# A scaled batched matmul with an addend: the last store moves into SyncE's list, and the program is closed while stores are in flight

## The chip, the cores and the metric

The kernel runs on one core of a Trainium2 chip. A core has five engines with an instruction stream each: TensorE (PE in the profile), VectorE (DVE), ScalarE (ACT), GpSimd (POOL) and SyncE (SP), which here does nothing but issue transfers and wait. Sixteen DMA engines move data between the memory of the chip and the core's SBUF. The streams meet only through semaphores. The metric is the device time of one execution in microseconds (us), as the median of several runs; lower is better.

## The reference

```python
def setup_inputs():
    batch, m, k, n = 16, 512, 1024, 768
    ...

def reference(x, weight, scale, add_value):
    return (scale * np.matmul(x, weight) + add_value).astype(np.float32)
```

All arrays are float32: `x` is 16x512x1024, `weight` 1024x768, `add_value` and the output 16x512x768, and `scale` is 0.1.

## The kernel before

The 16x512 rows are taken as one matrix of 8192 rows, cut into 64 tiles of 128 rows. `STREAM` lists, in the order in which SyncE issues them, loads of the weight (`w`), loads of `x` tiles (`x`), loads of addend tiles (`a`) and stores of finished tiles (`o`); an entry gives the first tile and the number of tiles. `sync_engine` walks this list. Ahead of each transfer, `need` puts a wait if SyncE hasn't yet waited for that value: for slots of `x` to be used up, for the store that leaves an addend slot free, or, ahead of a store, for VectorE's count of finished tiles, `made` (L140).

ScalarE and GpSimd (`mover`, L149 to L161) cast `x` to bfloat16 and lay it out, VectorE (`turn`, L171) transposes it, TensorE (`tensor_engine`, L216) multiplies it with the weight, which VectorE has cast, and VectorE (`finish`, L181) scales the product, adds the addend in place in `ao` and raises `made`. `ao` has 32 tile slots; a store reads straight from it. Each engine waits on semaphores whose values are written out by hand, so the order of the work is fixed by the kernel and not by a scheduler.

Two semaphores, `o_sem[0]` and `o_sem[1]`, are used for the stores in turn: store number i raises `o_sem[i % 2]` by 16 when it has landed, and from the third on it first waits until the store two places before it has (L139). The list ends with the stores of tiles 32 to 47 (6144 KB) and of tiles 48 to 59 (4608 KB). GpSimd issues three further, small stores of two tiles in the middle of the run (`store_pair`).

All this stands in one hand-ordered section (`tc.tile_critical`, L240). At its end the framework puts a meeting: SyncE raises a flag, each other engine drains, answers, and SyncE goes on when all have answered. Only then does SyncE issue the last store, of tiles 60 to 63 (1536 KB, `LAST`, L251 and L252), outside the section, with a semaphore that the framework chooses.

The framework's close follows, in a block of instructions of its own (shown as line 283, the launch's `with` statement). SyncE waits for the last store, the five engines meet at a barrier, GpSimd clears the semaphores of the program in one instruction, and the engines meet at a second barrier. There the program ends. Nothing waits by itself for the store of tiles 48 to 59.

Of the kernel before, what the change touches and what calls it, by code (L numbers as in the profile page):

```python
# [21 lines left out]
STREAM = [  # L22
# [5 lines left out]
]  # L28
FIRST, LAST = (0, 8), (60, 4)
PAIR, TURN_AT = slice(8, 16, 7), 2  # L30
BY_POOL = [(122, 6), (0, 98), (98, 24)]

# [2 lines left out]
def kernel(  # L35
# [8 lines left out]
    nc = tc.nc  # L44
# [14 lines left out]
    out_v = out_f.rearrange("(g p t) n -> p g t n", p=P, t=R)  # L59
    w_v = weight.rearrange("(c p r) n -> p c (r n)", p=P, r=2)  # L60

    def rows(view, s, n):
        assert s // R == (s + n - 1) // R
        return view[:, s // R, s % R:s % R + n, :]
# [5 lines left out]
    ao = const.tile([P, A_SLOTS, N], fp32, name="ao")  # L70
# [2 lines left out]
    xt = const.tile([P, XT_TILES, KC, P], fp32, name="xt")  # L73
    mm = psum.tile([P, MM_BUFS, 1024], fp32, name="mm")

    w_sem = [tc.alloc_semaphore(f"w{i}") for i in range(2)]
    x_sem = [tc.alloc_semaphore(f"x{i}") for i in range(X_SLOTS // MOVE)]
    a_sem = tc.alloc_semaphore("a")
    o_sem = [tc.alloc_semaphore(f"o{i}") for i in range(2)]
# [8 lines left out]
    def slot(t):  # L88
        return t % A_SLOTS
# [5 lines left out]
    def sync_engine(eng):  # L95
        groups, stores, known = 0, [], {}

        def need(sem, value):
            if known.get(sem, 0) < value:
                eng.wait_ge(sem, value)  # L100
                known[sem] = value

        for at, (op, s, n) in enumerate(STREAM):
            if at == SYNC_AT:
                eng.addr_align(HALF_BLOCK, offset=PAST, max_nops=0)
            last = s + n - 1
            if op == "w":
                dst = ao[:, W_AT + s:W_AT + s + n, :].rearrange("p (c r) n -> p c (r n)", r=2)
                move, sem = eng.dma_start(dst, w_v[:, s // 2:(s + n) // 2, :]), w_sem[s // 4]
            elif op == "x":  # L110
                k = s % X_SLOTS
                if last >= X_SLOTS:
                    moved = 8 * (last + 1 - X_SLOTS) // MOVE
                    need(by_act, moved)
                    need(by_pool, moved)
                move = eng.dma_start(xs[:, k:k + n, :], rows(x_v, s, n))  # L116
                sem = x_sem[k // MOVE]
            elif op == "a":
                if groups:
                    need(a_sem, 16 * groups)  # L120
                if last == A_SLOTS - 1:
                    need(casts, KJ)
                if s <= PAIR.start + A_SLOTS <= last:
                    need(aside_sem, 16 * len(BY_POOL))
                if s >= A_SLOTS:
                    i = next(j for j, (a, b) in enumerate(stores) if a <= last - 1 - A_SLOTS < a + b)
                    need(o_sem[i % 2], 16 * (i // 2 + 1))
                move = eng.dma_start(ao[:, slot(s):slot(s) + n, :], rows(add_v, s, n))  # L128
                sem = a_sem
                groups += 1  # L130
            elif op == "a+":
                need(a_sem, 16 * groups)
                eng.sem_inc(a_sem, 16 * (n // G - 1))
                groups += n // G - 1
                continue
            else:
                i = len(stores)
                if i > 1:
                    need(o_sem[i % 2], 16 * (i // 2))  # L139
                need(made, MADE + last + 1)  # L140
                move = eng.dma_start(rows(out_v, s, n), ao[:, slot(s):slot(s) + n, :])
                sem = o_sem[i % 2]
                stores.append((s, n))
            move.then_inc(sem, 16)
            if op == "x" and n == 2 * MOVE:
                eng.sem_inc(x_sem[k // MOVE + 1], 16)
# [69 lines left out]
    def tensor_engine(eng):  # L216
        eng.sem_inc(x_sem[1], 16)
        eng.sem_inc(turned, TURNED)
        eng.sem_inc(made, MADE)
        eng.wait_ge(casts, KJ)  # L220
        with eng.Fori(TURNED + 2, TURNED + 2 + T, XT_TILES) as i:
            for q in range(XT_TILES):
                if q % 2 == 0:
                    eng.wait_ge(turned, i + q if q else i)
                    eng.wait_ge(made, i + q if q else i)
                for j in range(KJ):
                    x2 = xt[:, q, j // 2, :].bitcast(bf16).rearrange("p (m r) -> p r m", r=2)
                    m = product(eng, mm[:, q, :], x2[:, j % 2, :], w_bf[:, j, :], j)
                if q % 2:
                    m.then_inc(done, 4)  # L230
# [4 lines left out]
    s, n = FIRST  # L235
# [4 lines left out]
    with tc.tile_critical(no_gpsimd_drain=True):  # L240
        sync_engine(nc.sync)
        mover(nc.scalar, nc.scalar.copy, 0, by_act)
        mover(nc.gpsimd, nc.gpsimd.tensor_copy, 1, by_pool, pool_go, 0, TURN_AT)
        nc.gpsimd.wait_ge(made, MADE + PAIR.stop)
        for p, n in BY_POOL:
            store_pair(nc.gpsimd, p, n)
        nc.gpsimd.addr_align(HALF_BLOCK, offset=PAST, max_nops=0)
        mover(nc.gpsimd, nc.gpsimd.tensor_copy, 1, by_pool, pool_go, TURN_AT, T // X_SLOTS - TURN_AT)
        vector_engine(nc.vector)
        tensor_engine(nc.tensor)  # L250
    s, n = LAST  # L251
    nc.sync.dma_start(rows(out_v, s, n), ao[:, slot(s):slot(s) + n, :])  # L252


# [33 lines left out]
```

## Time and profile before

| | |
|---|---|
| median of 3 runs | 208.18 us (208.1 to 208.29) |
| profiled execution, its own time | 208.1 us |
| span of that execution, first to last instruction | 206.3 us |
| TensorE busy | 168.5 us (82%) |
| GpSimd / ScalarE / VectorE busy | 137.4 / 134.7 / 98.0 us |
| moved by DMA | 87.04 MB, 422 GB/s over the span |
| mean granted TensorE clock | 0.981 |

The span counts from the first instruction of the program; all times of the trace are us from there. An engine's name with a q behind it (SPq, POOLq) means an instruction that its sequencer carries out by itself: a wait, a drain, a branch, the issue of a transfer. `L141` is line 141 of the kernel before. "To landing" is the time from the issue of a transfer until its semaphore has its full count. In a row of the view of windows stand the stretch, its length, busy time and instructions of each engine, then the granted clock, the mean busy share of the 16 DMA engines and GB/s. In a row of the view of one line stand the operation and count, its shortest, median and longest time in ns, and the start of the first and the last of them.

### The profile page before, as it was taken

To read this page: it belongs to the slowest core of one execution; us is meant where nothing else is said; L and a number is where in the kernel's file an instruction comes from. 1 tells how busy PE (TensorE), PEld (TensorE's weight loads), DVE (VectorE), ACT (ScalarE), POOL (GpSimd) and SP (SyncE) were. 2 spreads that over 40 slices of the span, in tenths; PEclk is the share of its full clock that TensorE was granted. 3 is DMA by queue.
4 is the path that set the end of the run, shared out by engine and by line. 5 is a ranking of instruction groups with operands and counts; after the bars stand their busy time and mean duration, and the time that the engine had idled before them with its cause. 6 is when DMAs were issued, how large, how long until landed. Compare 5 with 4: busy or idle time off the path is not lost.

```text
span 206.3 us, 2222 instructions
## 1 busy us (share of the span) xinstructions
PE 168.5 (82%) x1008; PEld 50.5 (24%) x512; DVE 98.0 (48%) x66; ACT 134.7 (65%) x129; POOL 137.4 (67%) x135
## 2 busy tenths in 40 slices
PE   0000099999999999999999999999999999999800
PEld 0000023322333333223333322233333222333200
DVE  0005523555555555555555555555554655455320
ACT  2049970799999807999999069999990199910000
POOL 0049994699999906999999459999991199920000
PEclk9999999999999999999999999999999999999975
DMA  7989999999999999999999999999999999999986
GB/s 299 413 378 467 400 483 407 419 438 464 407 457 457 407 407 407 407 457 408 437 434 423 447 424 434 432 419 443 438 415 429 429 437 443 429 457 419 457 367 281
DMA packets 4065, 87.04 MB, mean 422 GB/s; under 512 B 480, under 2 KB 480, under 8 KB 1120
## 3 DMA queue, kind: packets, MB, share of 16 engines
q1 hardware_dynamic: 3856, 86.25, 97.7%
q0 software_dynamic: 208, 0.79, 0.9%
q14 instruction: 1, 0.01, 0.0%
HBM read 61.87 MB, written 25.17 MB: 422 GB/s over the span
## 4 chain that ended last, share of the span: by engine, by line
DMA 37%; PE 37%; POOL 10%; ACT 5%; issue 4%; DVE 2%; SPq 1%; POOLq 0%; DVEq 0%; ACTq 0%
PE mm L208 37%; DMA out_dram<-ao 22%; DMA xs<-in_x_dram 15%; POOL va L161 9%; ACT va L161 5%; DVE xt L176 1%; DVE ao L185 1%; POOL out_dram L93 1%; SPq L128 0%; SPq L116 0%; DVEq L174 0%; SPq L100 0%; POOLq L154 0%; POOLq L151 0%; DVEq L185 0%
## 5 line engine op out<-in xcount | busy, mean ns | idle before, releaser
L208 PE MATMUL mm<-w_bf,xt 128*128 128x256 bf16 (+1 forms) x1008 | 168.5, 328 | 27.1 <-DVE xt L176 26.2
L161 POOL CAST va<-xs 32x1024 bf16<-32x1024 f32 x128 | 135.2, 1056 | 44.3 <-DMA xs<-in_x_dram 30.6
L161 ACT CAST va<-xs 32x1024 bf16<-32x1024 f32 x128 | 133.4, 1042 | 45.3 <-DMA xs<-in_x_dram 41.7
L185 DVE SCALAR_TENSOR_TENSOR ao<-mm,ao 128x1536 f32 (+1 forms) x32 | 56.2, 1757 | 76.7 <-PE mm L208 73.6
L206 PEld LDWEIGHTS <-xt 128*128 128x128 bf16 x512 | 50.5, 99 | 144.5 <-issue 117.6
L176 DVE STREAM_TRANSPOSE xt<-va 128x1024 f32<-128x1024 f32 x32 | 39.4, 1234 | 4.6 <-POOL va L161 2.4
L169 DVE CAST w_bf<-ao 128x3072 bf16<-128x3072 f32 x2 | 4.6, 2276 | 18.0 <-DMA ao<-in_weight_dram 18.0
L150 ACT ACT_TABLE_LOAD x1 | 1.3, 1283 | 1.3 <-SPq L240 1.3
L93 POOL DMA_DIRECT2D out_dram<-ao x3 | 2.0, 672 | 0.0
L269 POOL MEMSET const-float32-0.0<- 128x1 f32 x1 | 0.1, 97 | 0.2 <-issue 0.2
L269 POOL MEMSET const-bfloat16-1.0<- 128x1 bf16 x1 | 0.1, 100 | 0.0
L269 POOL MEMSET const-float32-1.0<- 128x1 f32 x1 | 0.1, 98 | 0.0
L269 POOL MEMSET const-uint8-127<- 128x1 uint8 x1 | 0.1, 98 | 0.0
## 6 DMA issues: line engine op xcount, KB each, us to landing
xs<-in_x_dram SPq DMA_DIRECT2D x7, 4096.0 KB, 20.9
ao<-in_add_value_dram SPq DMA_DIRECT2D x6, 3072.0 KB, 16.0
out_dram<-ao SPq DMA_DIRECT2D x3, 3072.0 KB, 27.4
ao<-in_add_value_dram SPq DMA_DIRECT2D x1, 6144.0 KB, 24.2
out_dram<-ao SPq DMA_DIRECT2D x1, 6144.0 KB, 31.2
out_dram<-ao SPq DMA_DIRECT2D x1, 4608.0 KB, 14.7
xs<-in_x_dram SPq DMA_DIRECT2D x2, 2048.0 KB, 21.1
ao<-in_weight_dram SPq DMA_DIRECT2D x2, 1536.0 KB, 16.8
```

The lines of the kernel that those rows point to most:

```text
L93: eng.dma_start(out_v[p:p + n, 0, PAIR, :], ao[p:p + n, PAIR, :]).then_inc(aside_sem, 16)
L150: eng.preload_act_table(mybir.ActivationFunctionType.Copy)
L161: copy(va[q % VA_BUFS][32 * b:32 * b + 32, :, a, :], src[32 * a:32 * a + 32, :, b, :]).then_inc(count, 1)
L169: eng.tensor_copy(w_bf[:, s:s + n, :], ao[:, W_AT + s:W_AT + s + n, :]).then_inc(casts, n)
L176: eng.transpose(xt[:, 2 * half:2 * half + 2, :, :].rearrange("p i c m -> p (i c m)"), va[move % VA_BUFS][:, q:q + 2 * KC, :, :].bitcast(fp ...
L185: eng.scalar_tensor_tensor(a, mm[:, q:q + 2, 0:N], float(scale), a, op0=mybir.AluOpType.mult, op1=mybir.AluOpType.add).then_inc(made, 2)
L206: eng.ldweights(x_j, tile_position=(0, 0))
L208: m = eng.add_instruction(mybir.InstMatmult(start_tensor_calc=(j == 0), stop_tensor_calc=(j == KJ - 1), tile_size=(P, P), tile_position=(0 ...
L269: nc = _bacc.Bacc("TRN2", target_bir_lowering=False, num_devices=1)
```

## The change

The last store becomes an entry of `STREAM`. The last two stores of the list, those from tile 48 on, raise a new semaphore, `ending`, that is not one of the framework's. Behind the section the kernel itself closes its pools, closes the context and compiles the program, and then adds one instruction to SyncE: wait until `ending` has reached 32, and take 32 off it.

```diff
     ("x", 60, 4), ("a", 56, 8), ("o", 32, 16), ("o", 48, 12),
+    ("o", 60, 4),
 ]
-FIRST, LAST = (0, 8), (60, 4)
+FIRST, ENDING = (0, 8), 48
...
+    end_sem = nc.alloc_semaphore("ending")
     w_sem = [tc.alloc_semaphore(f"w{i}") for i in range(2)]
...
                 need(made, MADE + last + 1)
                 move = eng.dma_start(rows(out_v, s, n), ao[:, slot(s):slot(s) + n, :])
-                sem = o_sem[i % 2]
+                sem = o_sem[i % 2] if s < ENDING else end_sem
                 stores.append((s, n))
...
         tensor_engine(nc.tensor)
-    s, n = LAST
-    nc.sync.dma_start(rows(out_v, s, n), ao[:, slot(s):slot(s) + n, :])
+    ctx.close()
+    tc.close()
+    tc.compile()
+    ending = 16 * sum(op == "o" and s >= ENDING for op, s, n in STREAM)
+    nc.sync.wait_ge(end_sem, ending).then_inc(end_sem, -ending)
```

In the built program the instructions of TensorE, VectorE, ScalarE and GpSimd are the same ones in the same order; the numbers of the semaphores shift by one, and GpSimd's clearing covers all but `ending`. On SyncE the last store stands inside the section, behind one wait for `made` and a wait of its own for `o_sem[0]` to reach 48, which is the landing of the store of tiles 32 to 47. The wait for the last store ahead of the first closing barrier is gone; the wait for `ending` stands behind the second.

## The prediction

> **What bounds the kernel now.** I read the page first, for the share of each engine, the transfer rates and the chain of waits.
>
> ```profile
> span 206.3 us, 2222 instructions
> DMA packets 4065, 87.04 MB, mean 422 GB/s; under 512 B 480, under 2 KB 480, under 8 KB 1120
> q14 instruction: 1, 0.01, 0.0%
> DMA 37%; PE 37%; POOL 10%; ACT 5%; issue 4%; DVE 2%; SPq 1%; POOLq 0%; DVEq 0%; ACTq 0%
> ```
>
> No engine is full; DMA moves 422 GB/s on average and shares the chain with TensorE. The change lies at the end, so I then followed the chain of waits in order of time to its last piece, the timeline of SyncE, and every DMA issue with its time to landing.
>
> ```profile
> 195.63 1.76 DVE ao L185
> ...
> 159.69 27.67 SPq L141 DMA_DIRECT2D out_dram<-ao  x2
> 197.67 0.33 SPq L252 DMA_DIRECT2D out_dram<-ao  x1
> ...
> 187.01 0.34 SPq L141 DMA_DIRECT2D out_dram<-ao  x1
> ...
> out_dram<-ao SPq DMA_DIRECT2D x1, 6144.0 KB, 31.2
> out_dram<-ao SPq DMA_DIRECT2D x1, 4608.0 KB, 14.7
> out_dram<-ao SPq DMA_DIRECT2D x1, 1536.0 KB, 7.7
> ```
>
> The chain stops at the last piece of compute, 195.63 + 1.76 = 197.39 us. The 8.9 us from there to 206.3 are the last store and the close, and the chain shows neither. The merged row of two stores starts at the first of them, 159.69; the second is the row at 187.01. So the last three stores land at 159.69 + 31.2 = 190.9, 187.01 + 14.7 = 201.7 and 197.67 + 7.7 = 205.4 us. What follows 205.4 is the closing code, line 283:
>
> ```profile
> L283 POOLq EVENT_SEMAPHORE  x4: 17/17/17, 205.6 to 206.2; - x4
> L283 SPq EVENT_SEMAPHORE  x3: 17/17/17, 205.4 to 206.2; - x3
> L283 PEldq EVENT_SEMAPHORE  x2: 51/51/51, 205.7 to 206.3; - x2
> L283 POOLq EVENT_SEMAPHORE_RANGE_CLEAR  x1: 161/161/161, 205.9 to 205.9; - x1
> ...
> SPq L283 <- DMA out_dram<-ao: 7.4, 1, 7.4
> ```
>
> SyncE waits 7.4 us for the last store (197.67 + 0.33 + 7.4 = 205.4). Only then do the five engines meet, GpSimd clears the semaphores (161 ns), they meet again, and the last of them, TensorE's, finishes at 206.3. So 206.3 - 205.4 = 0.9 us of closing stand behind the landing with nothing else running.
>
> **The close goes under the store.** In the changed kernel the same meeting, clearing and meeting are issued with both stores in flight, and SyncE alone waits behind them on a semaphore that the clearing leaves out. The closing work is the same, 0.9 us. Ahead of it stands the end of the hand-ordered section, whose length is the time from the last compute to the old store issue, 197.67 - 197.39 = 0.28 us: SyncE raises a flag, the others drain and answer. Before, that flag went up at 187.4; now it goes up behind the last issue, so the other four engines stand idle until then, with nothing left to do. The new order ends near 197.8 + 0.3 + 0.9 = 199.0 us, with 205.4 - 199.0 = 6.4 us to spare. What hides the close is the flight of the last store; with that cover gone it would cost its 0.9 us again, plus the 0.28. Removed from the path: 0.9 us.
>
> **Does the close really not wait for transfers?** The drains are what could. The trace has SyncE's drain standing right behind an issue, with that store in flight:
>
> ```profile
> L240 SPq DRAIN  x1: 53/53/53, 187.5 to 187.5; - x1
> ```
>
> It took 53 ns at 187.5, behind the issue of 187.01 to 187.35, and that store landed at 201.7. So a drain waits for the issue and not for the landing. I take zero; the other bound, a drain that holds to the landing, gives back the whole 0.9.
>
> **The last store's issue.** It now stands in SyncE's list. It waits for the last compute, then for the 6144 KB store, since two stores share each of the semaphores in turn, then it goes. The second wait was met at 190.9, 6.5 us before the first. Two rows of the chain price a wait instruction ahead of a transfer:
>
> ```profile
> 116.72 0.02 SPq L100
> 116.74 0.03 issue
> 116.77 0.38 SPq L116
> ```
>
> That is 0.05 us. A store that waits for compute directly went at 187.01, and its compute ended at 185.23 + 1.76 = 186.99, so 0.02 us of reaction. The new issue is at 197.39 + 0.02 + 0.05 = 197.46, 0.21 us earlier than 197.67. Behind the waiting store stands only the close, so nobody else is held.
>
> ```profile
> 185.23 1.76 DVE L185 SCALAR_TENSOR_TENSOR ao<-mm,ao 128x1536 f32<-128x1536 f32 x1 [1.99 <-PE mm L208]
> ```
>
> **What the earlier issue is worth.** Here I had to choose. Between the landings at 190.9 and 201.7, 4608 KB went out in 10.8 us, which is 437 GB/s; between 201.7 and 205.4, 1536 KB in 3.7 us, 425 GB/s. Both are the mean rate of the whole run (422) or above it. So the three stores run nose to tail through a full pipe. I checked whether the last one could have started sooner, by the first load of the program, issued at 0.74 us:
>
> ```profile
> 0.74 0.38 SPq L237 DMA_DIRECT2D xs<-in_x_dram  x1
> ...
> 0.74:1.50 0.76, 0.00 (x0) 0.00 (x0) 0.00 (x0) 0.16 (x1) 0.00 (x0) 1.00 0.00 0
> 1.50:2.00 0.50, 0.00 (x0) 0.00 (x0) 0.00 (x0) 0.50 (x1) 0.00 (x0) 1.00 2.05 590
> ...
> 199.60:199.80 0.20, 0.00 (x0) 0.00 (x0) 0.00 (x0) 0.00 (x0) 0.00 (x0) 0.50 2.56 1106
> 200.20:200.40 0.20, 0.00 (x0) 0.00 (x0) 0.00 (x0) 0.00 (x0) 0.00 (x0) 0.50 0.00 0
> ```
>
> The last two columns are the DMA share and GB/s. Nothing moved until 1.50 and packets began before 2.00, so an issue takes 0.76 to 1.26 us to its first packet. The last store was ready by 197.67 + 1.26 = 198.9 at the latest, yet was served from about 201.7 - 205.4: it stood 2 to 3 us in line. An empty window at 200.20 seems to speak against a full pipe. It doesn't: a share of 2.56 in 0.2 us is possible only if a packet's whole time is booked at its start, so empty windows are those in which no packet begins. Issuing 0.21 us earlier therefore lengthens the time in line, from 7.7 to about 7.9 us, and the landing stays at 205.4. What hides this part is the 4608 KB store ahead. I take 0 for it, between 0 and a gain of 0.21.
>
> The Trainium skill ("DMA: Bandwidth & Descriptors", in "Anatomy of one DMA") fits a transfer by itself as 2.0 us plus its bytes at 436 GB/s. By that estimate the last store would take 5.6 us, be bound by its issue and carry the 0.21 us to the end, for a gain of 1.1; the measured 7.7 us says that it waited about 2 us for others, so here the trace decides against it.
>
> **The new last wait.** One semaphore instruction of SyncE, 17 ns as in the row of line 283. Its count is 32, both stores; the 4608 KB one lands 3.7 us before the other, so it is never the later. Before, no wait was spent on it at all.
>
> **What lies around the span.** The profiled execution took 208.1 us, 1.8 more than its span, and the trace doesn't show how that is made up. The last engine still has to finish and report, so I leave the 1.8 as it is; the bounds are no change and one meeting of the engines saved, because four of them arrive early: half of the 0.9, 0.45 us.
>
> **Sum**, against the profiled execution: 208.1 - 0.9 (close) - 0 (issue) + 0.02 (wait) = 207.2 us. The median of the runs shown, 208.18, is 0.08 above that execution, so the forecast is 207.3 us, 0.4% faster. A change of less than 0.2%, 0.42 us, can't be told from none.
>
> **Rivals.**
>
> *The landing follows the issue.* If the DMA engines did run dry before the last store, its landing moves with the issue, to 205.2, and the gain is 0.9 + 0.21: 207.1 us. For it: the empty window at 200.20 if it is taken at its word. Against: the rates between the landings.
>
> *The time around the span shrinks as well.* Four engines stop near 199 us rather than at 206.3. If a meeting behind the program costs less for that, 0.45 more is saved: 206.85 us. Nothing in the trace speaks for or against.
>
> *The change doesn't do what it says.* If a drain or the clearing holds until the stores have landed, the 0.9 us stay behind the landing and SyncE's 0.02 comes on top: 208.2 us, no change. Against: the drain of 53 ns.
>
> *Slower: the closing code isn't there when it is wanted.* One mechanism: the jump into the closing block has to fetch its instructions through the same DMA engines, behind two stores. A small transfer in a full pipe can take long:
>
> ```profile
> out_dram<-ao POOLq DMA_DIRECT2D x1, 144.0 KB, 18.6
> ```
>
> A fetch held until the pipe empties arrives at 205.4, and the chain of 0.28 + 0.9 = 1.2 us then ends at 206.6, 0.3 later than before: 208.5, still within what can't be told. From a second fetch in series on, 1.0 us or so by the load at 0.74 us (between 0.76 and 1.26), it is slower: 209.5. For a single fetch, it decides when it takes over 6.4 us. For it: the closing code stands in a block of its own, reached by a jump. Against: the page has one instruction packet in the whole run, and ScalarE made the same jump in 0.1 us, from its drain at 187.4 to the one behind it at 187.5:
>
> ```profile
> L240 ACTq DRAIN  x1: 8/8/8, 187.4 to 187.4; - x1
> L283 ACTq DRAIN  x2: 8/8/8, 187.5 to 205.8; - x2
> ```
>
> The Trainium skill ("Runtime: NRT & Kernel Launch", in "Instruction fetch mechanics") says that a taken branch to a target outside the two blocks held forces a fetch by DMA before the engine goes on. By that rule the jump could stall; ScalarE's 0.1 us says that here the target was held.
>
> **How the numbers follow.** Forecast 68%, with a range of its own of 207.1 to 207.5 (rounding of 0.9 to a tenth, and the spread of the runs, 0.19 us). Landing follows the issue 12%, time around the span shrinks 7%, no change 8%, slower 5%. The first three are faster by over 0.2%: 0.87; same 0.08; slower 0.05. The range 206.8 to 207.75 takes in the first three, and leaves out the other two, 13%, and some of the tails.
>
> **What would show it.** Right: the span falls to 205.4; the events of the close stand between 197.8 and 199.5; the last instruction is SyncE's wait, at the landing; the last store is issued near 197.46, takes about 7.9 us, and lands at 205.4; the profiled execution still takes 1.8 us more than its span. Wrong: a landing near 205.2 (first rival); a difference between execution and span well below 1.8 (second); closing events at 205.4 or later (third); more instruction packets and gaps ahead of closing events (fourth).

## The result and the profile after

| | before | after |
|---|---|---|
| median | 208.15 us (208.07 to 208.29, 6 runs) | 207.05 us (206.85 to 207.14, 6 runs) |
| profiled execution, its own time | 208.1 us | 206.85 us |
| span of that execution | 206.3 us | 205.5 us |
| time less span in it | 1.8 us | 1.35 us |

After to before is 0.9941, with a 95% interval of 0.9931 to 0.9952: 1.1 us faster. The profiled execution of after is the fastest of its six; their spans run from 205.5 to 205.8 us.

From the page of the changed kernel and its view of transfers, the first line, the transfers of instructions, and the last two issues with their time to landing:

```profile
span 205.5 us, 2223 instructions
...
q14 instruction: 1, 0.01, 0.0%
...
out_dram<-ao SPq DMA_DIRECT2D x1, 4608.0 KB, 14.9
...
out_dram<-ao SPq DMA_DIRECT2D x1, 1536.0 KB, 8.1
```

The last piece of its chain of waits (start, length, what), and its timeline of SyncE behind that:

```profile
195.57 1.76 DVE ao L187
```

```profile
197.41 0.33 SPq L143 DMA_DIRECT2D out_dram<-ao  x1
```

The last compute ends at 195.57 + 1.76 = 197.33, and the last store is issued 0.08 us behind it, at 197.41; before it was 0.28 behind, at 197.67. It lands at 197.41 + 8.1 = 205.5. Before, it landed at 205.4 after 7.7 us. So it went out 0.26 us sooner and landed no sooner.

The view by line of the close (line 255 in this kernel; count, shortest/median/longest ns, first and last start) and of the new wait (line 257), and the row of SyncE's own waits for it:

```profile
L255 POOLq EVENT_SEMAPHORE  x4: 17/17/17, 198.3 to 198.9; - x4
...
L255 SPq DRAIN  x3: 7/7/7, 198.2 to 198.5; - x3
...
L255 PEldq EVENT_SEMAPHORE  x2: 51/51/51, 198.4 to 199.0; - x2
...
L255 POOLq EVENT_SEMAPHORE_RANGE_CLEAR  x1: 160/160/160, 198.6 to 198.6; - x1
```

```profile
L257 SPq EVENT_SEMAPHORE  x1: 17/17/17, 205.5 to 205.5; - x1
```

```profile
SPq L257 <- SPq L257: 6.5, 1, 6.5
```

The barriers and the clearing that stood at 205.6 to 206.3 now stand at 198.2 to 199.0, while both stores are in flight. SyncE then waits 6.5 us, and its wait at 205.5 is the last instruction. The view names SyncE itself as what ended this wait, since the instruction also takes 32 off the semaphore; it was the store.

The span of the profiled execution fell by 0.8 us. The other 0.45 us lie outside the span, where the trace shows nothing: an execution took 1.8 us more than its span before, and 1.35 (1.31 to 1.39 in six runs) after. By the medians, 1.1 us in all, it is 0.45 outside and 0.65 inside the span. Spans are recorded to 0.1 us, so the difference of a single run is good to 0.05.

The experiments went after both parts. For the second, the expectations below weigh three theories. Theory A: each engine has work of its own behind its last instruction, and of those that end late the slowest sets the time. Theory B: the engines meet once more behind the program, and the meeting costs less where four have been waiting. Theory C: the difference has nothing to do with when the engines end.

### The profile page after: what moved, and what is told of

It is laid out like the page before. It is cut to its first block, busy times and chain, and to the rows that moved or that the text cites. A ratio compares the mean times of both kernels' runs of the same rounds, so it can differ in the third digit from the quotient of the medians.

```text
span 205.5 us, 2223 instructions
## 1 busy us (share of the span) xinstructions
PE 167.5 (82%) x1008; PEld 50.4 (25%) x512; DVE 98.0 (48%) x66; ACT 134.7 (66%) x129; POOL 137.4 (67%) x135
## 4 chain that ended last, share of the span: by engine, by line
DMA 38%; PE 36%; POOL 10%; ACT 5%; issue 4%; DVE 3%; SPq 1%; POOLq 0%; DVEq 0%; ACTq 0%
PE mm L210 36%; DMA out_dram<-ao 22%; DMA xs<-in_x_dram 15%; POOL va L163 9%; ACT va L163 5%; DVE xt L178 2%; DVE ao L187 1%; POOL out_dram L95 1%; SPq L130 0%; SPq L118 0%; DVEq L176 0%; SPq L102 0%; POOLq L156 0%; POOLq L158 0%; POOLq L153 0%
```

## The experiments: the cover and the earlier issue

**The cover taken away.** SyncE waits for both stores at the end of the section, so that the end of the section and the close stand behind the landing; the last store keeps its earlier issue.

```diff
@@ sync_engine, behind the loop over STREAM
+        ending = 16 * sum(op == "o" and s >= ENDING for op, s, n in STREAM)
+        eng.wait_ge(end_sem, ending).then_inc(end_sem, -ending)
@@ behind the section
     tc.compile()
-    ending = 16 * sum(op == "o" and s >= ENDING for op, s, n in STREAM)
-    nc.sync.wait_ge(end_sem, ending).then_inc(end_sem, -ending)
```

> The changed kernel with the cover taken away: SyncE waits for both stores at the end of the hand-ordered section, so the section's end (0.28 us) and the close (0.9 us) stand behind the landing, and the last store keeps its earlier issue. By the prediction's steps: landing at 205.4 to 205.5, span 205.45 + 0.28 + 0.9 = 206.6 us; the rival by which the landing follows the issue has it 0.2 earlier, 206.4. The time less the span: 1.8 by theories A and B, since all five end together again, 1.35 by theory C. Time by A and B with the landing fixed 208.4, by C 208.0.

Measured: 208.69 us, 1.0021 of before (1.0011 to 1.003); the spans have a median of 206.9, and time less span is 1.83 (1.79 to 1.88). Its timeline of SyncE, its issues, and the view by line of the wait (line 150) and of the close (line 257):

```profile
197.48 0.33 SPq L143 DMA_DIRECT2D out_dram<-ao  x1
```

```profile
out_dram<-ao SPq DMA_DIRECT2D x1, 1536.0 KB, 7.9
```

```profile
L150 SPq EVENT_SEMAPHORE  x1: 17/17/17, 205.4 to 205.4; - x1
...
L257 POOLq EVENT_SEMAPHORE  x4: 17/17/17, 206.0 to 206.6; - x4
...
L257 PEldq EVENT_SEMAPHORE  x2: 51/51/51, 206.1 to 206.7; - x2
```

The landing is at 197.48 + 7.9 = 205.4, as before the change, although the issue is 0.19 sooner. From there to the last event are 1.3 us, against 0.28 + 0.9 expected. The time is 0.3 above the 208.4 that theories A and B had: the spans have a median of 206.9, where 206.6 was expected. With the close uncovered the whole gain is gone, and the end of the section comes on top: the kernel is slower than before. And time less span is back at before's value, so that part of the gain too hangs on when the engines end.

**The last store held back by two and by three transposes.** VectorE makes transposes behind its last compute, from a buffer that is done with into another, and the last store waits for them. Nothing reads what they write. `LATE` is 60, the first tile of the last store, and `late` a semaphore of its own; with three transposes both 2s are a 3.

```diff
                 need(made, MADE + last + 1)
+                if s == LATE:
+                    need(late, 2)
...
         group(2 * T, slice(s, s + 1), True)
+        for i in range(2):
+            if i:
+                eng.wait_ge(late, i)
+            eng.transpose(
+                xt[:, 0:2, :, :].rearrange("p i c m -> p (i c m)"),
+                va[0][:, 0:2 * KC, :, :].bitcast(fp32).rearrange("p c a k -> p (c a k)"),
+            ).then_inc(late, 1)
```

> The changed kernel with the last store held back: VectorE makes two further transposes behind its last compute (1.25 us each, and a wait between them), whose output nothing reads, and the last store waits for them. It is issued near 200.1 us in place of 197.4, 2.7 later. With a full pipe (the landing is set by the store ahead): the store is ready at 200.1 + 0.76 to 1.26 = 200.9 to 201.4, about when the last DMA engines come free, so the landing moves by 0 to 0.3 us, to 205.4 to 205.7, and time from issue to landing falls to about 5.4. If the landing follows the issue: 2.7 later, 208.1, span 208.2. A late issue that cost nothing would show that the 0.2 us by which the change issues earlier could not be worth anything either.

> As the run with two further transposes, with three: the last store is issued near 201.5 us, 4.1 later than in the changed kernel. With a full pipe up to then: it is ready at 202.2 to 202.7, past the end of the store ahead, so from here the landing follows: 0.9 to 1.4 us later than in the changed kernel, 206.3 to 206.9. If the landing follows the issue all along: 4.1 later, 209.5. If the store ahead had run longer than I think, nothing moves.

The timeline of VectorE and SyncE, the issues, and the last wait with two transposes:

```profile
197.21 2.51 DVE L212 STREAM_TRANSPOSE xt<-va 128x1024 f32<-128x1024 f32 x2
...
199.81 0.33 SPq L146 DMA_DIRECT2D out_dram<-ao  x1
...
out_dram<-ao SPq DMA_DIRECT2D x1, 1536.0 KB, 5.6
...
L267 SPq EVENT_SEMAPHORE  x1: 17/17/17, 205.4 to 205.4; - x1
```

And with three:

```profile
201.10 0.33 SPq L146 DMA_DIRECT2D out_dram<-ao  x1
...
out_dram<-ao SPq DMA_DIRECT2D x1, 1536.0 KB, 5.1
...
L267 SPq EVENT_SEMAPHORE  x1: 17/17/17, 206.2 to 206.2; - x1
```

With two, the store goes out at 199.81, 2.4 us later than in the changed kernel, and lands at 205.4: nothing is lost. The time is 206.93 us, 0.9937 of before (0.9921 to 0.9954), the same as the changed kernel's. With three it goes out at 201.10, 3.7 us later, lands at 206.2, and the time is 207.63 us (0.9973, interval 0.996 to 0.9986). Only then does the landing follow, by 0.7 us. I had expected 0.9 to 1.4 from an issue at 201.5; the transposes were done 0.4 sooner than that.

With three, the store finds the DMA engines nearly free, and takes 5.1 us from issue to landing. So a landing at 205.4 needs an issue by 205.4 - 5.1 = 200.3. The change issues at 197.41, before it was 197.67: both have 2.6 us or more to spare. The Trainium skill's fit for a transfer by itself ("DMA: Bandwidth & Descriptors", in "Anatomy of one DMA") gave an estimate of 5.6 us for this store. The section states that fit for transfers that GpSimd issues, and the prediction carried it over to one of SyncE's; the 5.1 measured here is near it and 0.5 shorter.

## The experiments: what lies around the span

**One engine ends last.** The wait behind the close is put on another engine; nothing else changes.

```diff
-    nc.sync.wait_ge(end_sem, ending).then_inc(end_sem, -ending)
+    nc.gpsimd.wait_ge(end_sem, ending).then_inc(end_sem, -ending)
```

(or `nc.tensor`, `nc.scalar`, `nc.vector`.)

> The changed kernel with the wait for both stores behind the close put on TensorE in place of SyncE. The other four end near 199 us. Theory A (own work behind each engine's last instruction): the time less the span is TensorE's own, which need not be 1.35; among TensorE, GpSimd, ScalarE and VectorE at least one shows about 1.8. Theory B (a meeting is cheaper where four wait): 1.35 whichever engine is the last. Theory C (nothing to do with who ends when): 1.35. The span grows by no more than 0.05 us, since TensorE's semaphore instructions take 51 ns and SyncE's 17.

> The changed kernel with the wait for both stores behind the close put on GpSimd in place of SyncE. Theory A: the time less the span is GpSimd's own; it was the engine that ran the barriers and the clearing, so I put it first among the candidates for 1.8. Theory B and theory C: 1.35. The span as in the changed kernel, 205.5 to 205.8 us, since GpSimd's semaphore instructions take 17 ns as SyncE's do.

> The changed kernel with the wait for both stores behind the close put on ScalarE in place of SyncE. Theory A: the time less the span is ScalarE's own, between below 1.35 and 1.8. Theory B and theory C: 1.35. The span 205.5 to 205.8 us. If it comes out below 1.3, this version beats the changed kernel.

> The changed kernel with the wait for both stores behind the close put on VectorE in place of SyncE. Theory A (own work behind each engine's last instruction): the time less the span is VectorE's own, between below 1.35 and 1.8. Theory B (a meeting is cheaper where four wait) and theory C (nothing to do with who ends when): 1.35. The span 205.5 to 205.8 us.

**Several engines end together.** SyncE waits for the stores, tells others one by one, and each told engine waits for its own semaphore as its last instruction.

```diff
     end_sem = nc.alloc_semaphore("ending")
+    others = (nc.tensor, nc.vector, nc.scalar, nc.gpsimd)
+    told = [nc.alloc_semaphore(f"told{i}") for i in range(len(others))]
...
     nc.sync.wait_ge(end_sem, ending).then_inc(end_sem, -ending)
+    for eng, sem in zip(others, told):
+        nc.sync.sem_inc(sem, 1)
+    for eng, sem in zip(others, told):
+        eng.wait_ge(sem, 1).then_inc(sem, -1)
```

> The changed kernel, with SyncE telling the four other engines when both stores have landed, and each of them waiting for it as its last instruction; so all five end together again, as before the change, but without a barrier or a clearing behind the landing. The time of an execution less its span was 1.8 us before the change (208.1 less 206.3) and is 1.31 to 1.39 us in six runs of the changed kernel. Theory A (each engine has work of its own behind its last instruction, SyncE's is the shorter, and the slowest of those that end late sets the time): the difference goes back to about 1.8. Theory B (the engines meet once more behind the program, and a meeting costs less where four have been waiting): back to about 1.8 too. Theory C (the difference has nothing to do with when the engines end: the clearing, the numbers of the semaphores, the closing block): it stays near 1.35. The span grows by 0.05 to 0.15 us for the telling (five semaphore instructions of 17 to 51 ns). Time by A and B 207.5 to 207.7, by C 207.1 to 207.2.

The next two differ in `others` alone: `(nc.gpsimd, nc.scalar, nc.vector, nc.tensor)`, and `(nc.tensor, nc.vector, nc.scalar)`.

> The run in which all five engines end together, with the order of telling turned round: GpSimd is told first, then ScalarE, VectorE and TensorE. Measured so far, the time less the span by the engine that ends alone: GpSimd 1.90, TensorE 1.62, ScalarE 1.47, VectorE 1.46, SyncE 1.35; with all five ending together and GpSimd told last 2.11, which is 0.2 more than GpSimd's own. By the ends in that run (told engines end 0.06 us apart) GpSimd should end near 205.60, ScalarE 205.66, VectorE 205.72, TensorE 205.82 and SyncE 205.74. Theory A alone (each engine's own tail, the latest counts): the latest is GpSimd, 205.60 + 1.90 = 207.5, less the span of 205.82, 1.68. Theory A with a shared step that the five pass one after another: GpSimd is now ahead of the others in it and the 0.2 goes, or another engine pays it: 1.7 to 1.85. Theory B (a meeting of all, paid when the last one arrives): as before the turning, 2.1.

> As the run in which all five engines end together, but GpSimd isn't told and ends near 199 us. Theory A alone: the latest is TensorE, ending near 205.64, and 1.62 behind it is 207.26; less the span of 205.72 it is 1.54. Theory A with a shared step: up to 0.2 more, 1.75. Theory B: 2.1, or little less for one engine fewer.

And `(nc.gpsimd,)` and `(nc.tensor,)`:

> The changed kernel with GpSimd alone told by SyncE that both stores have landed, so that two engines end late, GpSimd about 0.08 us behind SyncE. With several engines ending late the time less the span came out 0.13 to 0.26 us above what the single tails give (2.11 against 1.90 with GpSimd last of five, 1.94 against 1.68 with GpSimd first of five, 1.67 against 1.54 with four). If each engine's own tail is all there is: 1.90, GpSimd's. If the telling by a second semaphore costs the 0.2: 2.1. If it is the number of engines that end at once: 1.9 to 1.95, since there are only two.

> The same with TensorE in GpSimd's place. Own tails alone: 1.62, TensorE's. If the telling costs 0.2: 1.8. If it is the number of engines that end at once: 1.62 to 1.67.

Measured, with before and the changed kernel for comparison (medians; in brackets the lowest and highest of the runs):

| ends late | runs | time less span, us | span, us | time, us |
|---|---|---|---|---|
| SyncE (the changed kernel) | 6 | 1.35 (1.31 to 1.39) | 205.7 | 207.05 |
| VectorE | 4 | 1.46 (1.45 to 1.47) | 205.5 | 206.97 |
| ScalarE | 4 | 1.47 (1.46 to 1.55) | 205.5 | 206.97 |
| TensorE | 4 | 1.62 (1.61 to 1.67) | 205.6 | 207.22 |
| GpSimd | 8 | 1.90 (1.84 to 1.94) | 205.5 | 207.38 |
| SyncE, TensorE | 5 | 1.61 (1.59 to 1.67) | 205.8 | 207.40 |
| SyncE, GpSimd | 5 | 1.86 (1.85 to 1.91) | 205.7 | 207.55 |
| all but GpSimd | 6 | 1.67 (1.62 to 1.69) | 205.95 | 207.60 |
| all, GpSimd told first | 10 | 1.94 (1.91 to 2.01) | 205.9 | 207.83 |
| all, GpSimd told last | 10 | 2.11 (2.09 to 2.17) | 205.85 | 207.98 |
| all, behind the close (before) | 17 | 1.80 (1.75 to 1.87) | 206.3 | 208.14 |
| all, behind the close (the cover taken away) | 10 | 1.83 (1.79 to 1.88) | 206.9 | 208.69 |

The rows were measured at different times, with before at 208.14 to 208.28 beside them, so small differences in the last column are not a reading. With all told and GpSimd last, nothing clear of noise is left of the gain: 0.9991 of before (0.9982 to 1.0001).

The last events of the run in which GpSimd alone ends late, by line:

```profile
L257 POOLq EVENT_SEMAPHORE  x1: 17/17/17, 205.4 to 205.4; - x1
```

In this run the program ends at 205.4 as seen from the span, 0.1 us sooner than the profiled execution of the changed kernel, and yet the runs take 0.33 us longer than the changed kernel's (207.38 against 207.05; 0.9966 of before, 0.9955 to 0.9977, against 0.9941, 0.9931 to 0.9952). What follows an engine's last instruction depends on the engine: 1.35 us for SyncE, up to 1.90 for GpSimd. Theory B, a meeting that is cheaper where four wait, asked for 1.35 whichever engine is last, and falls; theory C, nothing to do with who ends when, falls with it and with the run without cover (1.83). Theory A stands: each engine has a time of its own behind its last instruction, a tail, and the latest end of a tail sets the time. Whether a tail is the engine's own work or, say, its place in a meeting that goes through the engines in a fixed order isn't told apart here: both would give each engine a figure of its own. The two pairs agree with theory A: 1.61 and 1.86 for 1.62 and 1.90. So it does not take five engines that end late to pay 1.9 us; it takes GpSimd.

Before the change GpSimd's last event is the row "205.6 to 206.2" shown in the prediction, and 206.2 + 1.90 = 208.1 us is the time that this execution took. The run with the cover taken away, which wasn't used to find the tails, gives the same: GpSimd's last event is at 206.6, and 206.6 + 1.90 = 208.5, where the execution took 208.52.

What stays open is a remainder in the runs in which three or four engines are told. The last event that counts, in the run with SyncE and TensorE, SyncE and GpSimd, all but GpSimd, all with GpSimd told first, and all with GpSimd told last, in this order:

```profile
L263 PEldq EVENT_SEMAPHORE  x1: 51/51/51, 205.7 to 205.7; - x1
```

```profile
L263 POOLq EVENT_SEMAPHORE  x1: 17/17/17, 205.7 to 205.7; - x1
```

```profile
L263 PEldq EVENT_SEMAPHORE  x1: 51/51/51, 205.8 to 205.8; - x1
```

```profile
L263 POOLq EVENT_SEMAPHORE  x1: 17/17/17, 205.8 to 205.8; - x1
```

```profile
L263 POOLq EVENT_SEMAPHORE  x1: 17/17/17, 205.8 to 205.8; - x1
```

Each start with its length and the engine's single tail, against the time of that execution:

| ends late | told | latest end of a tail, us | took, us | remainder |
|---|---|---|---|---|
| all, behind the close (before; the cover taken away) | none | 208.1; 208.5 | 208.10; 208.52 | 0 |
| SyncE, TensorE | 1 | 205.7 + 0.05 + 1.62 = 207.4 | 207.40 | 0 |
| SyncE, GpSimd | 1 | 205.7 + 0.02 + 1.90 = 207.6 | 207.59 | 0 |
| all but GpSimd | 3 | 205.8 + 0.05 + 1.62 = 207.5 | 207.59 | 0.1 |
| all, GpSimd told first | 4 | 205.8 + 0.02 + 1.90 = 207.7 | 207.91 | 0.2 |
| all, GpSimd told last | 4 | 205.8 + 0.02 + 1.90 = 207.7 | 207.91 | 0.2 |

So the remainder doesn't come from the number of engines that end at once by itself: five that end within 0.1 us behind the close show none. Telling one engine doesn't cost it either. It grows with the number of engines told; with all told and GpSimd last the time less span is 2.11, where theories A and B expected about 1.8. Turning the order round lowered the time less span from 2.11 to 1.94, but the remainder stayed, so it isn't a shared step with GpSimd at its end; 1.94 is what none of the three expectations for that run had (1.68; 1.7 to 1.85; 2.1). In the run with all but GpSimd, 1.67 is inside the range of a shared step (up to 1.75), above the 1.54 of tails alone. By which mechanism several tellings add to the time, these runs don't show.

None of the versions beats the changed kernel: with VectorE or ScalarE last 0.9941 of before each (0.9924 to 0.9958 and 0.9924 to 0.9957), and with two transposes 0.9937, all within the changed kernel's interval.

## Why the prediction came out as it did

The forecast was 207.3 us, and 207.05 was measured, within the stated range but 0.05 below the range of the likeliest case: it is inside only because the stated range was drawn to take in the first two rivals. By the number alone the first rival, at 207.1, would seem to be the one that came; the landing rules it out, as said below.

**The close under the store** was right. The close starts at 198.2 and ends at 199.0, the predicted end, and the run without cover gives back the gain. The 0.9 us showed up as 0.8 in the profiled span because this landing came 0.1 later (205.5). The end of the section took longer than the 0.28 us taken, from the end of the issue at 197.41 + 0.33 = 197.74 to 198.2, and under the store that cost nothing.

**The drain that doesn't wait for the landing** was right: in the changed kernel SyncE's drains of the close take 7 ns at 198.2 to 198.5, with stores in flight until 205.5.

**The earlier issue, worth 0,** was right, and here the first rival falls. An issue 0.26 us sooner moved nothing, and neither did one 2.4 us later. The choice rested on the rates between the landings; the empty window that spoke for the rival was, as argued, no idle pipe.

**The new last wait** was right: 17 ns, at the landing.

**What lies around the span** is the step that failed: "so I leave the 1.8 as it is". It fell by 0.45 us. The reason given, that the last engine still has to finish and report, is true as far as it goes; what it overlooked is that the time left then depends on the engine, and that the change also settles which engine is the last. The second rival had the size (0.45) and a chance of 7%, but its mechanism, a meeting that becomes cheaper, is not the one: GpSimd leaves the group that ends late, and SyncE has the shortest tail. Before, GpSimd ended 0.1 us ahead of the span's end, so 1.90 - 0.1 = 1.8 showed; after, SyncE's 1.35. That the difference is the rival's half of 0.9 is chance. The sum with this term as measured is 208.18 - 0.9 - 0.45 + 0.02 = 206.85; the measured 207.05 lies 0.2 above, by the later landings (spans of 205.5 to 205.8 where 205.4 was forecast). Whether the change itself makes the store land later, these runs don't show; three of the versions with another engine last have median spans of 205.5.

**The slower rival**, closing code that isn't there, didn't come: one instruction packet as before, and 0.8 us from SyncE's first drain of the close to TensorE's last event.

## What to carry to other kernels

Whatever the end of a program doesn't owe to the last transfer, barriers and clearing above all, can go in front of the landing, with one wait behind it; what it brings is what stood between the landing and the last event. Ask of an earlier issue whether the pipe is free to take it: add up the bytes between the last landings, or hold the issue back and see from when the end moves. And look at the time outside the span as well: it depends on which engine ends last.

## What the runs showed of the hardware that was not expected

The time behind a program's last instruction depends on the engine that ends last: 1.35 us where SyncE ends last, 1.46 and 1.47 for VectorE and ScalarE, 1.62 for TensorE, 1.90 for GpSimd, and up to 2.11 where SyncE tells all four others and the five end within 0.2 us. No view of a trace shows it; it appears only as the time of an execution less its span.
